# SwiGLU with a 128-byte gap ahead of its tiles, and with one weight split moved between the quarters of the gated parts

## The chip, the cores and the metric

The kernel runs on one core of one Trainium2 chip. The metric is device time in microseconds (us) of one execution of the whole program, the median of several runs. TensorE (PE in the profile) multiplies matrices, and its weight loads have a row of their own (PEld); VectorE is DVE, ScalarE is ACT, GpSimd is POOL, and SP only issues transfers.

## The reference, cut to what matters

The program is a two-layer decoder trunk on 512 tokens of width 1024, all in float32: a recurrent layer with its feed-forward part, then a dilated attention layer with its own feed-forward part. The change touches only the feed-forward part, which is run twice:

```python
def swiglu(h, w_in, w_out):              # h: 512 x 1024, hidden width 2816
    g, u = jnp.split(h @ w_in, 2, axis=-1)
    return (jax.nn.silu(g) * u) @ w_out
```

## The kernel before, in words

**Every product is three matmuls.** A float32 operand is split into a high part (rounded to the fp32r type of TensorE) and a low part (the rest). `mm3` at lines 161 to 165 then issues high times high (L163), high times low (L164, L165), with the first operand held in the array (the stationary one, which the weight load brings in) and the second streamed past it (the moving one). In the profile's names `ps<-gh,wh` the moving operand stands first and the stationary one second. Nearly all matmuls here have a stationary tile of 128x128 and a moving tile of 128x512.

**The stream of weights.** `Stream` (line 74) keeps weight pieces of 128x1024 floats. `_load` brings a piece from HBM into one of two raw buffers `wr`; `_split` makes its high part `wh` with a copy on ScalarE (L117) and its low part `wl` with a subtraction on VectorE (L124). There are three buffers each of `wh` and `wl`. `get(i)` is called just before the matmuls that use piece i, and first splits all pieces up to i + 2 (`asp` is 2 inside the feed-forward part). So the split of piece i + 3 is written into the program only at the `get` of piece i + 1.

**The feed-forward part.** `swiglu` (line 575) computes the first product in five quarters of 512 hidden columns and a plain remainder of 256 columns. A quarter uses a seven-product scheme on 2x2 blocks (`product`, line 739): combinations of the input, split into high and low parts, are the stationary operands, and combinations of the weights are the moving ones. Four of the input combinations (B11, B21, B22, T4) lie in the tiles `xh` and `xl` of the trunk's own pool; three (T1, T2, T3) lie in three tiles of the feed-forward pool, named T in the profile. The gated result of a quarter is transposed by VectorE into `wt`, and sixteen transfers (`land`, line 722) bring it into `gl`. `parts_of` (line 733) then makes its high part `gh` (a copy on ScalarE, L736) and its low part, in `gl` itself (a subtraction on VectorE, L737), in four quarters of 128x512 each. `out_block` (line 770) multiplies them by the second weight matrix: there the weights are stationary, and `gh` and `gl` are the moving operands. For the last quarter no `gh` and `gl` are used: the tiles T1 and T2 take the gated result, so that T is the moving operand in the last eight output blocks (line 814).

**The order.** Within `swiglu` all five engines run in the order in which the code issues (the manual schedule at line 788). The order of a quarter is a string (lines 40 to 42). In the middle ones it is "S1.T1 GA.B11 GB.B21 L S2.T2 O O S3.T3 O S4.B22 O UB.T4", where a name with a dot is a product of 24 matmuls, O is an output block of 24 matmuls, and L is `parts_of` for the quarter before. At an L the pieces for the following product S2 are already split, and the piece of the first O behind it is not: its split is written at the first `get` of S2, behind the four copies and four subtractions of the L. The two engines therefore do, in this order: for GB the additions (L707) and Silu (L708) of `gate`; the four quarters of L736 and L737; then L117 and L124 for the piece of the first O. Four quarters of each feed-forward part begin with such an L, eight in the program. The last quarter has a second L, behind two O, for the gated result that lies in T1 and T2.

**Where tiles lie.** A pool places its tiles in the order in which the code first asks for them, and a tile that is asked for and never used takes its place too. Sizes in bytes of a partition: the trunk's pool (h, xh, xl, constants) and the weights' pool (`wr`, `wh`, `wl`) hold only multiples of 512, so all of these start at the same address modulo 512; call that residue 0. The pool of the second feed-forward part follows directly. That of the first follows the pool "tables", whose tiles, with an unused one of 64 at its start (line 867), come to 64 + 1280 + 3072 + 3x64 + 512 + 1024 = 6144, twelve times 512. So both begin at residue 0. The order inside is: T1, T2, T3 and wt (8192 each), six temporaries e (4096 each), GA, GB, S1 (8192 each), then three small tiles of the norm in two buffers of 64 each (384 together), then S3, UB (8192 each), rb (3072), gh and gl (8192 each). Hence T, wt, e, GA, GB and S1 are at residue 0, and S3, UB, rb, gh and gl at residue 384. All slices that a matmul reads begin at multiples of 512 bytes within their tile.

Of the kernel before, what the change touches and what calls it, by code (L numbers as in the profile page):

```python
# [15 lines left out]
F32 = mybir.dt.float32  # L16
# [22 lines left out]

MIDDLE = "S1.T1 GA.B11 GB.B21 L S2.T2 O O S3.T3 O S4.B22 O UB.T4"  # L40
ORDERS = ["GA.B11 GB.B21 O S1.T1 S2.T2 O S3.T3 S4.B22 UB.T4", MIDDLE, MIDDLE, MIDDLE,
          "S1.T1 GA.B11 GB.B21 L S2.T2 O S3.T3 S4.B22 UB.T4 O O L O"]

C_AN, C_AF, C_KV, C_BN, C_BF, C_CB, C_GA, C_GX, C_LAM, C_CW = [8 * i for i in range(10)]
N_PAR = C_CW + 32
# [28 lines left out]
class Stream:  # L74
# [63 lines left out]
    def load_to(self, i):  # L138
        while self.nl < min(len(self.pieces), i + 1):
            for step in self._load(self.nl):  # L140
                step()
            self.nl += 1

    def prefetch(self, i):
        n = len(self.pieces)
        self.load_to(i + self.al)
        while self.ns < min(n, i + self.asp + 1):
            for step in self._split(self.ns):
                step()
            self.ns += 1  # L150

    def get(self, i):
        self.prefetch(i)
# [3 lines left out]
def trunk(tc, A, out):  # L157
# [11 lines left out]
    def add_pieces(aps, kind="", but=0):  # L169

        start = len(pieces)
        pieces.extend((a, "" if but and i % but == 0 else kind) for i, a in enumerate(aps))
        return start
# [7 lines left out]
    class Ffn:  # L181


        def __init__(self, wi, wo, gain):
            self.gain = gain
            self.wi, self.wo = A[wi], A[wo]
            self.split = None
            self.steps = []
            for j in range(2):
                self.steps += [("plain", j, b, add_pieces([self.wi[b]])) for b in (j, HB + j)]  # L190
            for q, names in enumerate(ORDERS):
                waiting = list(range(0, 8, 2 if q else 4))
                for name in names.split():
                    if name == "O":
                        m = waiting.pop(0)
                        if q:
                            w = self.wo[m:m + 2, :, 512 * q - 256:512 * q + 256]
                        else:
                            w = self.wo[m:m + 4, :, :256]
                        self.steps.append(("out", q, m, add_pieces([w.rearrange("b q c -> q b c")])))  # L200
                    elif name == "L":
                        self.steps.append(("parts",))
                    else:
                        first = len(pieces)
                        for kk in range(2):
                            pieces.append((None, lambda hi, lo, *a: self.split(*a, hi, lo), q, name, kk))
                        self.steps.append(("product", q, name, first))
            self.last = [add_pieces([self.wo[m][:, 128 * (HB - 4):128 * HB]]) for m in range(8)]
# [12 lines left out]
    with tc.tile_pool(name="keep", bufs=1) as kp, tc.tile_pool(name="wts", bufs=3) as wp, \  # L221
            tc.tile_pool(name="ps", bufs=1, space=PSUM) as pp:
        kp, wp = Pool(kp), Pool(wp)
        ws = Stream(tc, nc, wp, pieces, 2, 1)
# [113 lines left out]
        with tc.tile_pool(name="lru", bufs=2) as lp, \  # L338
# [50 lines left out]
            parts = [ws.get(0), ws.get(1)]  # L389
# [158 lines left out]
            for ms in ((0, 1), *((m,) for m in range(2, 8))):  # L548
                parts = [ws.get(p_aout + m) for m in ms]
# [25 lines left out]
        def swiglu(fp, p, after, meanwhile=iter(())):  # L575
            ws.asp, ws.al = 2, 9
            temps = Temps(fp)

            def chunk():
                return [fp.tile([128, 4, T], F32R, name=n, bufs=1) for n in ("gh", "gl")]  # L580
# [149 lines left out]
                        (nc.gpsimd if a == 0 else nc.sync).dma_start(  # L730
                            lo[32 * b:32 * b + 32, :, 128 * a:128 * a + 128].bitcast(F32), src[32 * a:32 * a + 32, :, b])

            def parts_of():
                hi, lo = chunks[max(chunks)]
                for m in range(4):
                    S.copy(hi[:, m], lo[:, m].bitcast(F32))  # L736
                    V.tensor_tensor(lo[:, m], lo[:, m].bitcast(F32), hi[:, m].bitcast(F32), ALU.subtract)  # L737

# [48 lines left out]
            E = mybir.EngineType  # L787
# [19 lines left out]
            with tc.manual_schedule(engines={mybir.EngineType.PE}):  # L807
                for ms in ((0, 1), *((m,) for m in range(2, 8))):
                    parts = [ws.get(p.last[m]) for m in ms]
# [9 lines left out]
        with tc.tile_pool(name="tables", bufs=1) as rp:  # L819
            rp = Pool(rp)  # L820
            with tc.tile_pool(name="ffn1", bufs=2) as fp:
                fp = Pool(fp)
                tables = []

                def make_tables():
                    tables.extend((yield from rotary(nc, A, rp, fp)))

                def after_f1(m, ps):
                    V.tensor_tensor(by_time(h[m]), by_time(h[m]), in_turn(ps), ALU.subtract)
                    split(h[m], gain(C_KV, m), xh[m], xl[m])  # L830
                    squares(m, Temps(fp))

                swiglu(fp, p_f1, after_f1, make_tables())


            with tc.tile_pool(name="att", bufs=2) as ap:
                ap = Pool(ap)
                attention(tc, A, ap, ws, dict(locals()))

        with tc.tile_pool(name="ffn2", bufs=2) as fp:  # L840
            fp = Pool(fp)

            def after_f2(m, ps):

                halves = [(slice(0, 2), nc.scalar), (slice(2, 4), nc.sync)]
                for c, queue in halves if m == 7 else [(slice(0, 4), nc.sync)]:
                    x = by_time(h[m])[:, :, c]
                    V.tensor_tensor(x, x, in_turn(ps)[:, :, c], ALU.subtract)
                    c = slice(128 * c.start, 128 * c.stop)
                    queue.dma_start(out[m][:, c], h[m][:, c])  # L850

            swiglu(fp, p_f2, after_f2)
# [534 lines left out]
```

## Time and profile before

| what | value |
|---|---|
| median of 3 runs (lowest to highest) | 1164.31 us (1163.48 to 1164.59) |
| the profiled execution's own time | 1163.49 us |
| its span, first to last instruction | 1161.4 us |
| PE busy | 1151.7 us, 99% |
| PEld busy | 951.7 us, 82% |
| DVE busy | 851.1 us, 73% |
| ACT busy | 623.2 us, 54% |
| POOL busy | 186.2 us, 16% |
| granted TensorE clock, mean | 0.999 |

The span is cut by the profile into instructions of each engine. A matmul's row gives its modelled duration, about 0.39 us here, and consecutive matmuls overlap: the next one starts about 0.23 us after the one before. So the cost of a matmul to the program is the step from its start to the next start, and a matmul whose modelled duration is 5 ns longer also makes the next one start about 5 ns later. In a row of groups stand line, engine, operation, names, shapes and count, and behind the bar the busy time in us and the mean in ns. In a row of the timeline stand start and duration in us.

### The profile page before, as it was taken

How to read it: one execution, taken by the hardware profiler on the slowest of the kernel's cores; microseconds unless marked ns; L12 is line 12 of the kernel's file. 1: busy time of each engine (PE TensorE's matmuls, PEld its weight loads, DVE VectorE, ACT ScalarE, POOL GpSimd, SP SyncE). 2: the span in 40 equal slices, each digit the busy share in tenths (PEclk: the TensorE clock that was granted, in tenths of full speed). 3: DMA queues.
4: the chain of work that ended last, by engine and by line, in shares of the span. 5: the costliest groups of instructions: out<-in, count | busy, mean ns of one | idle time of the engine just before them, and what ended most of it. 6: DMA issues, size and time to landing. Idle time of an engine off the chain costs nothing.

```text
span 1161.4 us, 15131 instructions
## 1 busy us (share of the span) xinstructions
PE 1151.7 (99%) x5403; PEld 951.7 (82%) x5403; DVE 851.1 (73%) x1525; ACT 623.2 (54%) x901; POOL 186.2 (16%) x221
## 2 busy tenths in 40 slices
PE   9999999999999999999999999999999999999998
PEld 6788888888888888888888888898888888888887
DVE  7988678868777676887565667765888676676764
ACT  6797455553535353665555768665555435353522
POOL 4210010201001000020411234341102011011000
PEclk9999999999999999999999999999999999999999
DMA  7644366966665722333988658535669665657324
GB/s 242 152 113 113 101 227 161 242 190 162 179 174 167 196 73 77 123 104 92 218 191 173 156 104 199 117 74 110 224 162 229 188 163 180 177 164 194 77 65 134
DMA packets 92234, 179.61 MB, mean 155 GB/s; under 512 B 8704, under 2 KB 27008, under 8 KB 92160
## 3 DMA queue, kind: packets, MB, share of 16 engines
q1 hardware_dynamic: 72720, 130.80, 34.9%
q0 software_dynamic: 18864, 47.19, 23.0%
q8 instruction: 43, 0.70, 0.2%
q10 hardware_dynamic: 576, 0.66, 0.2%
q14 instruction: 31, 0.25, 0.1%
HBM read 164.99 MB, written 2.10 MB: 144 GB/s over the span
## 4 chain that ended last, share of the span: by engine, by line
PE 94%; DVE 2%; ACT 1%; DMA 1%; issue 1%; POOL 0%; ACTq 0%; DVEq 0%; SPq 0%
PE ps L165 25%; PE ps L164 25%; PE ps L163 25%; PE ps L1048 6%; PE ps L1049 6%; PE ps L1050 6%; PE ps L1216 1%; PE ps L1134 1%; DVE xc L451 1%; DMA h<-in_x 0%; PE ps L296 0%; DMA wr<-in_w_in 0%; ACT pr L1202 0%; DVE xp L441 0%; PE ps L1102 0%
## 5 line engine op out<-in xcount | busy, mean ns | idle before, releaser
L117 ACT CAST wh<-wr 128x1024 fp32r<-128x1024 f32 (+2 forms) x136 | 131.2, 970 | 135.8 <-PE ps L164 81.0
L164 PE MATMUL ps<-wl,xh 128*128 128x512 f32 x320 | 124.6, 389 | 0.0
L165 PE MATMUL ps<-wh,xl 128*128 128x512 f32 x320 | 124.5, 389 | 0.0
L163 PE MATMUL ps<-wh,xh 128*128 128x512 f32 x320 | 124.5, 389 | 0.0
L165 PE MATMUL ps<-gh,wl 128*128 128x512 f32 x288 | 114.5, 398 | 0.3
L163 PE MATMUL ps<-gh,wh 128*128 128x512 f32 x288 | 113.6, 395 | 0.0
L164 PE MATMUL ps<-gl,wh 128*128 128x512 f32 x288 | 113.6, 394 | 0.0
L124 DVE TENSOR_TENSOR wl<-wr,wh 128x1024 fp32r<-128x1024 f32 (+2 forms) x93 | 100.0, 1084 | 16.8 <-ACT wh L117 16.4
L649 POOL DMA_DIRECT2D S<-in_f_in x40 | 48.2, 1247 | 368.9 <-DMA S<-in_f_in 186.6
L163 PE MATMUL ps<-xh,wh 128*128 128x512 f32 x256 | 101.0, 396 | 0.6 <-ACT xh L274 0.6
L663 ACT CAST wh<-S 128x1024 fp32r<-128x1024 f32 x60 | 63.0, 1050 | 70.4 <-PE ps L165 27.9
L164 PE MATMUL ps<-xl,wh 128*128 128x512 f32 x256 | 100.2, 391 | 0.1
L165 PE MATMUL ps<-xh,wl 128*128 128x512 f32 x256 | 99.8, 390 | 0.0
L664 DVE TENSOR_TENSOR wl<-S,wh 128x1024 fp32r<-128x1024 f32 x60 | 73.2, 1222 | 31.4 <-ACT wh L663 31.4
L163 PE MATMUL ps<-wh,T 128*128 128x512 f32 x240 | 93.5, 390 | 0.0
L165 PE MATMUL ps<-wh,T 128*128 128x512 f32 x240 | 93.5, 390 | 0.0
L164 PE MATMUL ps<-wl,T 128*128 128x512 f32 x240 | 93.4, 389 | 0.0
L1048 PE MATMUL ps<-wh,xh 128*128 128x512 f32 x224 | 91.5, 408 | 0.0
L1050 PE MATMUL ps<-wh,xl 128*128 128x512 f32 x224 | 87.7, 391 | 0.0
L1049 PE MATMUL ps<-wl,xh 128*128 128x512 f32 x224 | 87.3, 390 | 0.0
L781 DVE TENSOR_TENSOR h<-h,ps 128x512 f32<-128x512 f32 x64 | 43.3, 685 | 54.9 <-PE ps L165 54.9
L163 PEld LDWEIGHTS ps<-wh,xh 128*128 128x128 f32 x320 | 60.1, 188 | 12.6
(284 smaller groups left out, 2669.5 us busy)
## 6 DMA issues: line engine op xcount, KB each, us to landing
S<-in_f_in SPq DMA_DIRECT2D x40, 512.0 KB, 6.4
S<-in_f_in POOLq DMA_DIRECT2D x40, 512.0 KB, 9.0
wr<-in_f_out SPq DMA_DIRECT2D x36, 512.0 KB, 5.3
wr<-in_w_q SPq DMA_DIRECT2D x28, 512.0 KB, 6.5
wl<-in_w_q POOLq DMA_DIRECT2D x28, 512.0 KB, 7.7
GA<-in_f_in SPq DMA_DIRECT2D x20, 512.0 KB, 4.9
GB<-in_f_in SPq DMA_DIRECT2D x20, 512.0 KB, 7.0
UB<-in_f_in SPq DMA_DIRECT2D x20, 512.0 KB, 5.3
```

Source lines behind the costliest of these rows:

```text
L117: nc.scalar.copy(hi[:, c], r[:, c])
L124: a = eng.tensor_tensor(lo[:, c], r[:, c], hi[:, c].bitcast(F32), ALU.subtract)
L163: PE.matmul(ps, wh, xh, start=first, stop=False, skip_group_check=on)
L164: PE.matmul(ps, wh, xl, start=False, stop=False, skip_group_check=on)
L165: PE.matmul(ps, wl, xh, start=False, stop=last, skip_group_check=on)
L649: nc.gpsimd.dma_start(c, p.part(1, q, n == "S1", i), accum_op=ALU.add)
L663: S.copy(hi, r)
L664: V.tensor_tensor(lo, r, hi.bitcast(F32), ALU.subtract)
L781: V.tensor_tensor(by_time(x), by_time(x), in_turn(ps), ALU.subtract)
L1048: PE.matmul(ps[t], xh[k][:, r], wh[:, c], start=k == 0, stop=False)
L1049: PE.matmul(ps[t], xh[k][:, r], wl[:, c], start=False, stop=False)
L1050: PE.matmul(ps[t], xl[k][:, r], wh[:, c], start=False, stop=k == 7)
```

## The change

Two edits. The first asks, at the start of `swiglu`, for a tile of 32 floats per partition (128 bytes) that nothing uses. The second adds to `Stream` a method that splits the next piece, and has `parts_of` call it between its second and its third quarter at every L of the order strings. The last quarter's second L becomes an E, which does the quarters as before and splits nothing. No other order and no transfer is written differently.

```diff
-          "S1.T1 GA.B11 GB.B21 L S2.T2 O S3.T3 S4.B22 UB.T4 O O L O"]
+          "S1.T1 GA.B11 GB.B21 L S2.T2 O S3.T3 S4.B22 UB.T4 O O E O"]
...
+    def split_one(self):
+        for step in self._split(self.ns):
+            step()
+        self.ns += 1
+
     def prefetch(self, i):
         n = len(self.pieces)
         self.load_to(i + self.al)
         while self.ns < min(n, i + self.asp + 1):
-            for step in self._split(self.ns):
-                step()
-            self.ns += 1
+            self.split_one()
...
-                    elif name == "L":
-                        self.steps.append(("parts",))
+                    elif name in "LE":
+                        self.steps.append(("parts", name == "L"))
...
         def swiglu(fp, p, after, meanwhile=iter(())):
             ws.asp, ws.al = 2, 9
             temps = Temps(fp)
+            fp.tile([128, 32], F32, name="gap", bufs=1)
...
-            def parts_of():
+            def parts_of(split_next):
                 hi, lo = chunks[max(chunks)]
                 for m in range(4):
+                    if m == 2 and split_next:
+                        ws.split_one()
                     S.copy(hi[:, m], lo[:, m].bitcast(F32))
                     V.tensor_tensor(lo[:, m], lo[:, m].bitcast(F32), hi[:, m].bitcast(F32), ALU.subtract)
```

By the order of requests the gap moves every tile of the two feed-forward pools by 128 bytes: T, wt, e, GA, GB and S1 from residue 0 to 128, and S3, UB, rb, gh and gl from 384 to 512, which is residue 0.

## The prediction

> **What bounds the kernel now.** I read the engines' busy times first, then TensorE's groups by shape, and then one place in the timeline.
>
> ```profile
> PE 1151.7 (99%) x5403; PEld 951.7 (82%) x5403; DVE 851.1 (73%) x1525; ACT 623.2 (54%) x901; POOL 186.2 (16%) x221
> ```
>
> TensorE is busy for all but 10 us of the span. A change can only help by making a matmul's step shorter or by taking away one of the few waits. So the groups of matmuls (busy us, mean ns of one):
>
> ```profile
> core 0 of [0], span 1161.4 us
> line engine op names shapes xcount | busy us, mean ns | idle before us <-releasers
> L164 PE MATMUL ps<-wl,xh 128*128 128x512 f32 x320 | 124.6, 389 | 0.0
> ...
> L165 PE MATMUL ps<-gh,wl 128*128 128x512 f32 x288 | 114.5, 398 | 0.3
> L163 PE MATMUL ps<-gh,wh 128*128 128x512 f32 x288 | 113.6, 395 | 0.0
> L164 PE MATMUL ps<-gl,wh 128*128 128x512 f32 x288 | 113.6, 394 | 0.0
> ...
> L163 PE MATMUL ps<-wh,T 128*128 128x512 f32 x240 | 93.5, 390 | 0.0
> L165 PE MATMUL ps<-wh,T 128*128 128x512 f32 x240 | 93.5, 390 | 0.0
> L164 PE MATMUL ps<-wl,T 128*128 128x512 f32 x240 | 93.4, 389 | 0.0
> ...
> L164 PE MATMUL ps<-T,wh 128*128 128x512 f32 x64 | 24.9, 389 | 0.0
> ```
>
> The same shape costs 389 to 390 ns everywhere, except where the gated product is the moving operand: 394 to 398 ns. That holds whether transfers run beside it or not. Here are two stretches, first by engine (the last two columns are DMA share and GB/s), then one group of matmuls from each:
>
> ```profile
> 185.60:191.10 5.50, 5.50 (x25) 4.42 (x24) 3.72 (x5) 2.28 (x3) 0.00 (x0) 1.00 0.04 7
> 267.50:272.20 4.70, 4.70 (x22) 3.85 (x21) 2.48 (x5) 1.98 (x2) 0.00 (x0) 1.00 1.02 256
> ```
>
> ```profile
> L163 PE MATMUL ps<-gh,wh 128*128 128x512 f32 x8 | 3.2, 395 | 0.0
> ```
>
> ```profile
> L163 PE MATMUL ps<-wh,xh 128*128 128x512 f32 x6 | 2.3, 390 | 0.0
> ```
>
> In the first stretch DMA is at 0.04 and gh matmuls take 395 ns. In the second DMA is at 1.02 and the xh ones take 390 ns, at the same granted clock of 1.00. Nor is it the code of the output block: with T in gh's place the same block takes 389 ns. What is left is where gh and gl lie. They are the only operands of such matmuls whose residue (384) is not that of the operand on the other side (0); T and xh stand at 0 like the weights.
>
> The other thing is a wait at every L. Matmul starts at the first one:
>
> ```profile
> 245.57 0.39 PE L165 MATMUL ps<-wh,T 128*128 128x512 f32 x1
> 245.80 0.39 PE L163 MATMUL ps<-gh,wh 128*128 128x512 f32 x1
> 246.03 0.40 PE L164 MATMUL ps<-gl,wh 128*128 128x512 f32 x1
> 246.47 0.50 PE L165 MATMUL ps<-gh,wl 128*128 128x512 f32 x1
> 246.81 0.39 PE L163 MATMUL ps<-gh,wh 128*128 128x512 f32 x1
> 247.04 0.39 PE L164 MATMUL ps<-gl,wh 128*128 128x512 f32 x1
> ...
> 249.83 0.39 PE L164 MATMUL ps<-gl,wh 128*128 128x512 f32 x1
> ```
>
> The third matmul of the first output block starts 0.44 us after the second, and the fourth 0.34 us after the third, where a step is otherwise 0.23. Among those who waited for the raw weights' split stands, over the whole program:
>
> ```profile
>   PEld ps L165: 3.7, 8
> ```
>
> The weight load of that third matmul waits for `wl`, eight times, once per L. ScalarE and VectorE at the same place:
>
> ```profile
> 242.03 2.17 ACT L736 CAST gh<-gl 128x512 fp32r<-128x512 f32 x4
> 244.11 2.00 ACT L117 CAST wh<-wr 128x1024 fp32r<-128x1024 f32 x2
> ```
>
> ```profile
> 242.67 2.50 DVE L737 TENSOR_TENSOR gl<-gl,gh 128x512 fp32r<-128x512 f32 x4 [1.31 <-ACT gh L736]
> 245.19 2.36 DVE L124 TENSOR_TENSOR wl<-wr,wh 128x1024 fp32r<-128x1024 f32 x2
> 248.03 1.22 DVE L664 TENSOR_TENSOR wl<-S,wh 128x1024 fp32r<-128x1024 f32 x1 [0.49 <-ACT wh L663]
> ```
>
> VectorE begins the first `wl` at 245.19, only when all four quarters of gl are done, and at 2.36 / 2 = 1.18 us each ends it at 246.37. The matmul that needs it would have started at 246.03 + 0.23 = 246.26. The second `wl` is for a later block and not yet needed.
>
> **The change part by part. First, the split between the quarters.** It adds no instruction and no transfer; it moves one L117 and one L124 ahead of the last two quarters. ScalarE's copies step by (244.11 - 242.03) / 4 = 0.52 us, VectorE's subtractions by (245.19 - 242.67) / 4 = 0.63. ScalarE then does two quarters from 242.03, the weights from 243.07 to 244.1, and the other two quarters until 245.2; its second weight copy then ends at 244.11 + 2.00 = 246.11, as before. The copy needs the third `wh` buffer, free since the last matmul of GB; Silu, ahead on the same engine, already waits for GB's results, so no new wait arises. VectorE does two quarters until 243.93, idles until `wh` is there at about 244.15, makes `wl` until 245.35, and the last quarters until 245.98 and 246.61. Who waits for those? The weight load needs `wl` at 246.26: 0.9 us early. The moving gl of k = 2 is needed seven steps after 245.80, at 247.4, and is there at 245.98; that of k = 3 at 248.07, there at 246.61. The second `wl` ends at 246.61 + 1.18 = 247.79, before VectorE's next work at 248.03, which waits for ScalarE anyway. The raw buffer comes free about a microsecond sooner, so SP issues its reload sooner; nothing on that queue is pushed back. So the whole wait goes: 0.44 + 0.34 - 2 x 0.23 = 0.32 us, eight times, **-2.6 us**. Bounds: if only the late start counts, 8 x 0.21 = 1.7; if the part that the weight load waited came back whole, 3.7, of which I keep 3.0, since two starts show less.
>
> **Second, the gap, for gh and gl.** They come to the weights' residue. Their 864 matmuls took 113.6 + 113.6 + 114.5 = 341.7 us, of which 8 x 0.11 = 0.9 is the long third one above; 340.8 / 864 = 394.4 ns against 389.3. By starts, 247.04 to 249.83 is 12 steps of 232.5 ns, and undisturbed steps of products are 227 (the last fence below). The difference is 5.1 to 5.5 ns; I take 5.3: 864 x 5.3 = **-4.6 us**.
>
> **Third, the gap, for T.** It moves T from residue 0 to 128, away from the weights. T is stationary in 720 matmuls (three rows of 240) and moving in 192. The trace shows no matmul of this shape with such a pair, so I bound it. Is the loss a matter of the moving operand's own address, or of the pair? The steps just behind a group of gh matmuls speak for the pair:
>
> ```profile
> 257.26 0.40 PE L163 MATMUL ps<-wh,T 128*128 128x512 f32 x1
> ...
> 259.57 0.39 PE L164 MATMUL ps<-wl,T 128*128 128x512 f32 x1
> 259.80 0.39 PE L165 MATMUL ps<-wh,T 128*128 128x512 f32 x1
> ...
> 262.07 0.39 PE L163 MATMUL ps<-wh,T 128*128 128x512 f32 x1
> ```
>
> Both pairs of rows span ten steps inside one product whose operands are all at residue 0. The first ten take 2.31 us, the second ten 2.27. Whatever gh disturbs outlasts gh by ten matmuls: a phase between the two streams, the moving operand and the weights being loaded, rather than a property of gh's address. Of gh against the weights, the moving operand starts 128 bytes below the stationary one, modulo 512. Of the weights against the moved T, the moving one (0) again starts 128 below the stationary one (128). It is the same pair, shifted. So I price it like gh: 720 x 5.3 = **+3.8 us**; from below, nothing (+0). Where T is moving, it stands 128 above the weights, the other way round, which no row shows: between 0 and 192 x 5.3 = 1.0; I take the middle, **+0.5 us**. The other moved tiles (wt, e, GA, GB, S1, S3, UB, rb) are read and written by VectorE, ScalarE and transfers, which have slack except at an L, where it is about 1 us; I price them at nothing.
>
> **Sum:** -2.6 - 4.6 + 3.8 + 0.5 = -2.9 us. The profiled execution had 1163.49 us, span 1161.4 and about 2 around it, which the change leaves; it would become 1160.6. It lies 0.8 below the median shown, 1164.31, and the same difference there gives **1161.4 us**. With the bounds of the wait (-3.0 to -1.7), of the step (5.1 to 5.5 ns on a net 144 matmuls, 0.7 to 0.8) and of the moving T (0 to 1.0), the likeliest case reaches from 1160.5 to 1163.0.
>
> The Trainium skill says of TensorE, in "TensorE: Matmul & The Clock Gate", section "Step-by-step: what each phase is for", that it has two independent read ports, so that loading the next tile's weights takes no read bandwidth from the running matmul. By that rule no residue could matter between the two streams, and only the wait would go. The rows of gh (394 to 398 ns against 389) don't fit it unless something else slows gh.
>
> **The rivals.**
>
> *A stationary operand may lie anywhere.* If only the moving operand's address counts, T costs nothing in the 720. Then -2.6 - 4.6 + 0.5 = -6.7 us: 1157.6 (1157.1 to 1158.1 with the two ends for the moving T). For it: every slow row has gh or gl as the moving operand. Against it: the ten slow steps behind gh.
>
> *The residue is not the cause, or the gap takes no place.* Then the change does half of what it says, and gh stays at 394 ns for a reason not seen here. Only the wait goes: 1164.31 - 2.6 = 1161.7. Against it: T in the same code at 389 ns, and quiet and busy transfers alike. That an unused tile takes its place shows in the first feed-forward part, where T comes right only with the 64 unused bytes of "tables".
>
> *Slower: T pays more than gh did.* Weights stream against T in 720 matmuls, with the weight load turning between T's two halves of a product. The change wins 2.6 + 4.6 = 7.2 us elsewhere; spread over 720 + 192 matmuls of T that is 7.9 ns each, and from there it decides. The longest gh matmul was 404 ns:
>
> ```profile
> L163 PE MATMUL ps<-gh,wh x288: 390/393/404, 185.6 to 1135.1; 128*128 128x512 f32 x144
> ```
>
> That is 15 ns above 389; if all of T's ran so, 912 x 15 = 13.7, and the time is 1170.8; at 10 ns it is 1166.2. Against it: none of the three gh groups has a mean above 398 ns, 9 over the rest, and T's pair is gh's own.
>
> **How the numbers follow.** The likeliest case (T pays like gh) has 52%, the free stationary operand 22%, no effect of the residue 13%, slower T 9%; 4% are left for gains and losses that cancel (1164.3). A measurement of this kernel can tell about 0.2%, 2.3 us, from no change, so faster begins below 1162.0 and slower above 1166.6. Of the likeliest case two thirds lie below 1162.0 (35 of 52), of the second all but one (21), of the third 8: 64% faster. Slower is 7 from T and 1 for what I don't see: 8%. The rest, 28%, is no change. The range goes from the second rival's lower end, 1157.0, to 1164.4, past the likeliest case's upper end and the cancelling case; outside are most of the slower rival and a part of the ends.
>
> **What would show it.** The gh and gl rows at 389 to 390 ns; the rows `wh,T` and `wl,T` at about 395 (at 389 the first rival is right, above 398 the last); `T,wh` between 389 and 395; no PEld waiting eight times for `wl`, and steps of 0.23 us at the first O behind each L. If gh stays at 394, the residue is wrong. If the gaps at the L remain, look whether ScalarE's copy of the weights started late. The prediction is wrong most easily at the price of T's new residue, which stands on one pair seen the other way round.

## The result, and the profile after

The changed kernel takes 1160.79 us (1160.62 to 1162.09), beside 1163.48 us (1162.55 to 1165.77) for the kernel before on the same chip: a ratio of 0.9978, 95% interval 0.9969 to 0.9987, or 2.7 us less. The forecast was 2.9 us less: 1161.4 us, from a median of 1164.31.

The page of the changed kernel, its first line:

```profile
span 1158.7 us, 15131 instructions
```

The span is 2.7 us shorter with the same number of instructions. The groups of TensorE by shape (the lines of `mm3` are three higher than before):

```profile
L168 PE MATMUL ps<-gh,wl 128*128 128x512 f32 x288 | 112.2, 389 | 0.0
L167 PE MATMUL ps<-gl,wh 128*128 128x512 f32 x288 | 112.1, 389 | 0.0
L166 PE MATMUL ps<-gh,wh 128*128 128x512 f32 x288 | 112.0, 389 | 0.0
...
L166 PE MATMUL ps<-wh,T 128*128 128x512 f32 x240 | 94.9, 396 | 0.0
L168 PE MATMUL ps<-wh,T 128*128 128x512 f32 x240 | 94.8, 395 | 0.0
L167 PE MATMUL ps<-wl,T 128*128 128x512 f32 x240 | 94.7, 395 | 0.0
...
L168 PE MATMUL ps<-T,wl 128*128 128x512 f32 x64 | 25.3, 395 | 0.0
L166 PE MATMUL ps<-T,wh 128*128 128x512 f32 x64 | 25.3, 395 | 0.0
L167 PE MATMUL ps<-T,wh 128*128 128x512 f32 x64 | 25.3, 395 | 0.0
```

The rows of gh and gl, which stood between 394 and 398 ns, are down at 389. Those of T went from 389 or 390 up to 395 or 396, as the stationary and as the moving operand alike. The slowness has changed its place. Now the first output block behind the first L, as the starts of its matmuls:

```profile
245.62 0.39 PE L166 MATMUL ps<-gh,wh 128*128 128x512 f32 x1
245.85 0.40 PE L167 MATMUL ps<-gl,wh 128*128 128x512 f32 x1
246.08 0.39 PE L168 MATMUL ps<-gh,wl 128*128 128x512 f32 x1
246.31 0.39 PE L166 MATMUL ps<-gh,wh 128*128 128x512 f32 x1
...
248.35 0.39 PE L166 MATMUL ps<-gh,wh 128*128 128x512 f32 x1
```

The steps of 0.44 and 0.34 us are gone; all are 0.23. From 246.31 to 248.35 are nine steps of 227 ns, where the kernel before had 232.5. VectorE at the same place:

```profile
242.33 1.29 DVE L743 TENSOR_TENSOR gl<-gl,gh 128x512 fp32r<-128x512 f32 x2 [1.32 <-ACT gh L742]
243.80 1.23 DVE L124 TENSOR_TENSOR wl<-wr,wh 128x1024 fp32r<-128x1024 f32 x1 [0.18 <-ACT wh L117]
244.95 1.29 DVE L743 TENSOR_TENSOR gl<-gl,gh 128x512 fp32r<-128x512 f32 x2
```

The first `wl` is done at 245.03, 1.05 us before the matmul that needs it; the last quarters of gl end at 246.24. Over the whole program, those who waited for the split of the raw weights are now these, and no PEld is among them:

```profile
  POOL wl L121: 127.0, 32
  ACT wh L117: 27.0, 11
  DVE wl L124: 18.1, 40
```

A useful clock for all that follows is the length of a middle quarter, from the first gh matmul behind one L to the first behind the next. It holds seven products and four output blocks, 11 x 24 = 264 matmuls, of which 72 have T stationary and 96 have gh or gl moving. The next such start, before and after:

```profile
306.60 0.39 PE L163 MATMUL ps<-gh,wh 128*128 128x512 f32 x1
```

```profile
305.96 0.39 PE L166 MATMUL ps<-gh,wh 128*128 128x512 f32 x1
```

Before it is 306.60 - 245.80 = 60.80 us, after it is 305.96 - 245.62 = 60.34.

### The profile page after: what moved, and what is told of

It is laid out like the page before. It is cut to its first block, busy times and chain, and to the rows that moved or that the text cites. A ratio compares the mean times of both kernels' runs of the same rounds, so it can differ in the third digit from the quotient of the medians.

```text
span 1158.7 us, 15131 instructions
## 1 busy us (share of the span) xinstructions
PE 1150.0 (99%) x5403; PEld 953.4 (82%) x5403; DVE 851.0 (73%) x1525; ACT 622.9 (54%) x901; POOL 187.7 (16%) x221
## 4 chain that ended last, share of the span: by engine, by line
PE 94%; DVE 2%; ACT 1%; issue 1%; POOL 0%; DMA 0%; SPq 0%; DVEq 0%; ACTq 0%
PE ps L168 25%; PE ps L167 25%; PE ps L166 25%; PE ps L1054 6%; PE ps L1055 6%; PE ps L1056 6%; PE ps L1222 1%; PE ps L1140 1%; DVE xc L454 1%; PE ps L299 0%; DMA wr<-in_w_in 0%; ACT pr L1208 0%; PE ps L1108 0%; ACT wh L117 0%; DVE wl L124 0%
## 5 line engine op out<-in xcount | busy, mean ns | idle before, releaser
L168 PE MATMUL ps<-gh,wl 128*128 128x512 f32 x288 | 112.2, 389 | 0.0
L167 PE MATMUL ps<-gl,wh 128*128 128x512 f32 x288 | 112.1, 389 | 0.0
L166 PE MATMUL ps<-gh,wh 128*128 128x512 f32 x288 | 112.0, 389 | 0.0
L166 PE MATMUL ps<-wh,T 128*128 128x512 f32 x240 | 94.9, 396 | 0.0
L168 PE MATMUL ps<-wh,T 128*128 128x512 f32 x240 | 94.8, 395 | 0.0
L167 PE MATMUL ps<-wl,T 128*128 128x512 f32 x240 | 94.7, 395 | 0.0
L787 DVE TENSOR_TENSOR h<-h,ps 128x512 f32<-128x512 f32 x64 | 43.3, 685 | 49.6 <-PE ps L168 49.1
```

Of the source, the lines that this page charges most:

```text
L166: PE.matmul(ps, wh, xh, start=first, stop=False, skip_group_check=on)
L167: PE.matmul(ps, wh, xl, start=False, stop=False, skip_group_check=on)
L168: PE.matmul(ps, wl, xh, start=False, stop=last, skip_group_check=on)
L787: V.tensor_tensor(by_time(x), by_time(x), in_turn(ps), ALU.subtract)
```

## The experiments

### The two edits apart

The split alone leaves out this line of the change:

```diff
-            fp.tile([128, 32], F32, name="gap", bufs=1)
```

> The split between the quarters alone, without the gap. Theory (the prediction's sum): the eight waits go and nothing else, 8 x 0.32 = 2.6 us less than the kernel before; gh and gl rows stay at 394 ns, T rows at 389 to 390. Rival (the split's place gains little, and nearly all of the change's 2.7 us came from the gap): less than 0.7 us less, and steps at the first output block behind an L that are still 0.44 and 0.34 us.

Measured: 1160.92 us against 1163.8 for the kernel before, ratio 0.9974 (0.9964 to 0.9985), 2.9 us less. One row of its groups and two starts:

```profile
L166 PE MATMUL ps<-gh,wh 128*128 128x512 f32 x288 | 113.7, 395 | 0.0
```

```profile
245.73 0.40 PE L166 MATMUL ps<-gh,wh 128*128 128x512 f32 x1
...
306.23 0.40 PE L166 MATMUL ps<-gh,wh 128*128 128x512 f32 x1
```

gh stays at 395 ns, and the quarter is 60.50 us: 0.30 less than before, where 0.32 was priced. So the split alone is as fast as the whole change.

The gap alone adds only that line to the kernel before.

> The gap alone, without the split. Theory (gh and T pay alike, by the pair): 864 x 5.3 = 4.6 us won at gh, (720 + 192) x 5.3 = 4.8 us lost at T, so within 0.5 us of the kernel before; the eight waits stay. Rival (the gap is what made the change faster): about 2.7 us less than before.

Measured: 1163.16 us, ratio 0.9994 (0.9985 to 1.0003): no difference that can be told, 0.6 us by the medians. The wait is still there, but shorter:

```profile
245.55 0.39 PE L163 MATMUL ps<-gh,wh 128*128 128x512 f32 x1
245.78 0.40 PE L164 MATMUL ps<-gl,wh 128*128 128x512 f32 x1
246.06 0.50 PE L165 MATMUL ps<-gh,wl 128*128 128x512 f32 x1
246.40 0.40 PE L163 MATMUL ps<-gh,wh 128*128 128x512 f32 x1
```

```profile
306.07 0.39 PE L163 MATMUL ps<-gh,wh 128*128 128x512 f32 x1
```

The two steps are 0.28 and 0.34, so the wait costs 0.28 + 0.34 - 2 x 0.23 = 0.16 us instead of 0.32. The product S2.T2, which runs while the weights are split, has T stationary. Its 24 matmuls are now 6 ns slower each, 0.14 us in all, and `wl` is that much less late: VectorE ends it at 245.96, 0.41 us after the first of these starts, where it was 246.37 - 245.80 = 0.57 us in the kernel before. The quarter is 306.07 - 245.55 = 60.52. So in the changed kernel, with its quarter of 60.34, the split is worth 0.18 us per quarter and not 0.32.

### Both operands in place

The gap is asked for behind T, just ahead of rb; the split stays:

```diff
             temps = Temps(fp)
-            fp.tile([128, 32], F32, name="gap", bufs=1)
...
                 elif b == HB:
+                    fp.tile([128, 32], F32, name="gap", bufs=1)
                     rows[:] = [spread(*rows, fp.tile([128, 768], F32, name="rb", bufs=1)[:, :T], S.copy)]
```

> Split and gap, but the gap is asked for just before rb, behind T, wt, e, GA, GB, S1, S3 and UB: T stays at residue 0 and gh and gl come to residue 0 as well. Theory (every pair at one residue is fast): gh, gl and T rows all at 389 to 390 ns, 2.6 + 4.6 = 7.2 us less than before, 4.5 less than the changed kernel. Rival (gh became fast for another reason than its own residue, such as the moved raw weights GA and S1 or the temporaries): gh stays at 394 ns and only the 2.6 us of the waits are won.

Measured: 1155.37 us, ratio 0.9926 (0.9913 to 0.9938), 8.4 us less than before. This version beats both kernels.

```profile
L166 PE MATMUL ps<-gh,wh 128*128 128x512 f32 x288 | 112.0, 389 | 0.0
...
L166 PE MATMUL ps<-wh,T 128*128 128x512 f32 x240 | 93.4, 389 | 0.0
```

```profile
246.63 0.39 PE L166 MATMUL ps<-gh,wh 128*128 128x512 f32 x1
...
306.47 0.39 PE L166 MATMUL ps<-gh,wh 128*128 128x512 f32 x1
```

All rows of gh, gl and T are at 389 ns, and the quarter is 59.84 us, 264 steps of 226.7 ns with nothing between them. It won 1.2 us more than the 7.2 expected. Against the split alone the quarter lost 60.50 - 59.84 = 0.66 us; over the 96 matmuls of gh and gl that is 6.9 ns each, where 5.3 was priced. Over all 864 matmuls of the two traces the mean step of gh and gl went from 233.1 to 226.7 ns, so 6.4 of it is their own, more than the twelve steps and the rows of the kernel before told. The rest is the disturbance that outlasts gh in the products behind it.

### Is it the pair or the address?

The same kernel with every tile 128 bytes higher:

```diff
+        kp.tile([128, 32], F32, name="shift")
         h = [kp.tile([128, T], F32, name=f"h{k}") for k in range(KB)]
```

> The kernel with the gap behind T, and 128 unused bytes at the start of the trunk's own pool, so that every tile of the program lies 128 bytes higher, all operands of the matmuls at one common residue that differs from before. Theory (only the difference between the moving and the stationary operand's residue counts): all rows as with the gap behind T, 389 to 390 ns, time within 0.5 us of it. Rival (the absolute residue of an operand counts): all the matmuls of 512 columns, some 4600, pay 5 ns, and the time is 23 us longer than with the gap behind T.

Measured: 1154.79 us, ratio 0.9924 (0.9912 to 0.9937).

```profile
245.01 0.39 PE L166 MATMUL ps<-gh,wh 128*128 128x512 f32 x1
...
304.85 0.39 PE L166 MATMUL ps<-gh,wh 128*128 128x512 f32 x1
```

The rows of gh, gl and T are at 389 ns and the quarter is 59.84 us again. Moving all operands together by 128 bytes changes nothing, while moving T or gh alone by 128 does; so it is the operands' difference that counts.

### How the price goes with the distance

In both kernels here gh and gl stay at residue 0, and an unused tile ahead of T sets T's residue, another one in each feed-forward part. For the first of the two:

```diff
             temps = Temps(fp)
+            shift = 64 if p is p_f1 else 256
+            fp.pool.tile([128, shift // 4], F32, name="gap_t", bufs=1)
...
+                    fp.pool.tile([128, (640 - shift) // 4 % 128 or 128], F32, name="gap", bufs=1)
```

> The kernel with the gap behind T (gh and gl at residue 0), and T moved: to residue 64 in the first feed-forward part, to 256 in the second. How does the price go with the distance? Theory (any unequal residue costs the same): T rows at about 395 ns in both parts, so 912 x 6 ns = 5.5 us longer than with the gap behind T alone. Rival (only a distance of 128 to either side collides, four places of 128 bytes modulo 512): T rows at 389 ns at 256, and nearly so at 64; the time within 1.5 us of the gap behind T.

Measured: 1158.33 us, ratio 0.9953 (0.9930 to 0.9975). T's groups in the first part (T at 64), then in the second (T at 256):

```profile
L166 PE MATMUL ps<-wh,T 128*128 128x512 f32 x120 | 47.5, 396 | 0.0
...
L167 PE MATMUL ps<-T,wh 128*128 128x512 f32 x32 | 12.6, 394 | 0.0
```

```profile
L166 PE MATMUL ps<-wh,T 128*128 128x512 f32 x120 | 46.7, 389 | 0.0
...
L167 PE MATMUL ps<-T,wh 128*128 128x512 f32 x32 | 12.5, 389 | 0.0
```

Both theories fall. With T stationary a distance of 64 costs as much as 128, and a distance of 256 costs nothing in either role. So the residue that counts is modulo 256, not 512. With T moving, 64 costs less: the row of T with wl was at 389 ns and the other two at 393 and 394. Why is open.

The second kernel has 32 and 384 in place of 64 and 256.

> As the run before, with T at residue 32 in the first feed-forward part and at 384 in the second. With T at 384 the stationary T stands 128 below the moving weights, the other sign than in the changed kernel. Theory (any unequal residue costs the same): T rows at about 395 ns in both. Rival (the price grows with the distance or depends on the sign): T rows nearer to 389 ns at 32, and at 384 other values for the stationary and the moving T than the 395 of the changed kernel.

Measured: 1161.7 us, ratio 0.9983 (0.9972 to 0.9994). T at 32, then T at 384:

```profile
L167 PE MATMUL ps<-wl,T 128*128 128x512 f32 x120 | 47.4, 395 | 0.0
...
L166 PE MATMUL ps<-T,wh 128*128 128x512 f32 x32 | 12.7, 395 | 0.0
```

```profile
L167 PE MATMUL ps<-wl,T 128*128 128x512 f32 x120 | 47.4, 395 | 0.0
...
L166 PE MATMUL ps<-T,wh 128*128 128x512 f32 x32 | 12.6, 395 | 0.0
```

32 costs the full price in both roles, and so does 384. For 384 that is what modulo 256 says, since it is then 128. The times agree with the rows: 8.4 us less than before with both parts of T in place, 5.8 with one (the kernel with 64 and 256), 2.4 with none.

### Own weights or the next ones?

With the gap behind T, 128 unused bytes stand between the buffers of `wh` and of `wl`:

```diff
         hi = self.pool.tile([128, 1024], F32R, name=f"wh{i}", tag="wh")
+        if i == 0:
+            self.pool.tile([128, 32], F32, name="apart", bufs=1)
         lo = self.pool.tile([128, 1024], F32R, name=f"wl{i}", tag="wl")
```

> Which of a matmul's neighbours makes the pair: the weights already in the array, or the ones loaded while it runs? The kernel with the gap behind T, and 128 unused bytes between the buffers of wh and those of wl. Now xh, xl and wh are at residue 0, and wl, T, gh, gl and all that lies behind are at 128. In the first layer's first product xh and xl move and the weights are stationary, in turn xh with wh, xl with wh, xh with wl. Theory one (the load of the next weights collides with the stream): xl with wh is slow, since wl is loaded while it runs, at about 395 ns, and xh with wl is fast. Theory two (the own weights count): xh with wl is slow and xl with wh is fast. In the output blocks gh and gl move at 128: by theory one gh with wh and gh with wl are slow and gl with wh fast; by theory two gh with wh and gl with wh are slow and gh with wl fast. If the disturbance lasts several matmuls whatever began it, all three rows lie between. Longer in all than with the gap behind T: a third to two thirds of the first layer's 768 and of the 864 matmuls, the 720 with T stationary and the weights' high part moving, and the 320 with xh stationary and wl moving pay about 6 ns, some 8 to 12 us.

Measured: 1176.19 us, ratio 1.0103 (1.0074 to 1.0132), 20.8 us longer than with the gap behind T in the other comparison, about twice what was expected.

```profile
L168 PE MATMUL ps<-wh,xh 128*128 128x512 f32 x320 | 126.9, 397 | 0.0
L169 PE MATMUL ps<-wl,xh 128*128 128x512 f32 x320 | 126.4, 395 | 0.0
L170 PE MATMUL ps<-wh,xl 128*128 128x512 f32 x320 | 125.5, 392 | 0.0
L170 PE MATMUL ps<-gh,wl 128*128 128x512 f32 x288 | 114.1, 396 | 0.0
L169 PE MATMUL ps<-gl,wh 128*128 128x512 f32 x288 | 113.7, 395 | 0.0
L168 PE MATMUL ps<-gh,wh 128*128 128x512 f32 x288 | 113.4, 394 | 0.0
```

Neither theory has its fast row here: all three rows of gh pay 5 to 7 ns. The rows in which `xh` and `xl` move, for which the two theories were set apart, are these; they hold the first layer's product and the other products of that form:

```profile
L170 PE MATMUL ps<-xh,wl 128*128 128x512 f32 x256 | 102.2, 399 | 0.0
L169 PE MATMUL ps<-xl,wh 128*128 128x512 f32 x256 | 102.1, 399 | 0.1
L168 PE MATMUL ps<-xh,wh 128*128 128x512 f32 x256 | 102.0, 400 | 0.8 <-ACT xh L279 0.8
```

In the kernel moved as a whole they were at 390, 391 and 396. So `xh,wl`, whose own weights lie apart, and `xl,wh`, during which such weights are loaded, are both slow; their median step is 234 and 232 ns. That of `xh,wh`, whose mean holds a few long matmuls in both kernels, stays at 227, and its row pays least. Here either of the two seems to be enough. But the row `wh,xh` above has its own operands at residue 0, and the weights loaded beside it too, and is the slowest of its three at 397. And where T is stationary the other way round happens:

```profile
L168 PE MATMUL ps<-wh,T 128*128 128x512 f32 x240 | 94.2, 393 | 0.0
L170 PE MATMUL ps<-wh,T 128*128 128x512 f32 x240 | 93.8, 391 | 0.0
L169 PE MATMUL ps<-wl,T 128*128 128x512 f32 x240 | 93.2, 389 | 0.0
```

`wl,T`, both at 128, pays nothing between two rows of unequal residues, and these pay 4 and 2 ns, not 6. A matmul can thus pay for residues that belong to its neighbours, and need not; no rule tried here covers all of these rows, and whether the own weights or the next ones begin the loss stays open.

## Why the prediction was right, and where its sizes were off

**The forecast held:** 2.9 us less was said, 2.7 was measured, and the likeliest case was the one that happened.

**The split.** Priced at 2.6 us for eight waits; alone it measured 2.9 us and 0.30 us per quarter. The reordered work ran as worked out: `wl` 1.05 us early (0.9 was said). What the sum missed is that the edits share this term. With the gap, the product ahead of the wait is slower and the wait is only 0.16 us, so the split adds 0.18 us per quarter there, eight quarters with an L making about 1.4 us, not 2.6; the other 1.3 is won by the gap itself.

**gh and gl.** Priced at 4.6 us. The three groups went from 341.7 to 112.2 + 112.1 + 112.0 = 336.3 us, that is 5.4, of which 0.9 was the long third matmul of the wait: 4.5. By starts it is more: over both whole traces the 864 steps took 201.4 us with the split alone and 196.1 with the gap added, 5.3 us or 6.1 ns each. The modelled durations understate the step here, so this term was priced too small.

**T stationary.** Priced at 3.8 us on the ground that it is gh's pair shifted by 128. The groups went from 280.4 to 94.9 + 94.8 + 94.7 = 284.4: 4.0. The kernel moved as a whole shows that this ground was sound: the difference counts. That it is a matter of the moving operand and of the weights being loaded beside it, as the prediction says, is not shown; the run with `wl` apart leaves that open.

**T moving.** Priced at 0.5, between 0 and 1.0. It measured 3 x (25.3 - 24.9) = 1.2 us, outside the bound. The step that failed is the middle between two ends: the other sign is no other case, since 128 above and 128 below are the same modulo 256.

**How the terms add up.** Added from start to next start over both traces, the matmuls of gh and gl, which hold the waits too, took 203.6 us before and 196.1 after: 7.5 less, where 2.6 + 4.6 = 7.2 was priced. T stationary took 163.6 and 167.6, T moving 43.3 and 44.6: 5.3 more, where 4.3 was priced. That leaves 2.2 us. The other 0.5 lies in matmuls which the change does not touch, and these scatter: the matmuls with `xh` and `xl` moving in `mm3` alone took between 178.5 and 180.0 us in the kernels before, changed, and of the first four experiments. So the terms were off by 0.3 us one way and 1.0 the other, and the untouched matmuls made up for most of it. The terms were the right ones, with the right signs; that the forecast came within 0.2 us is luck.

**One reading was too wide.** The prediction says that this shape costs 389 to 390 ns everywhere but at gh and gl. In the kernel before, the rows `xh,wh` (396), `wh,xh` of line 1048 (408) and `wh,xp` (404) have the same shape and are longer still. Their medians are 389, so a few long matmuls of up to 499 ns make these means, while all of `gh,wh` lie at 390 or above with a median of 393. The three rows stay where they are after the change (398, 408, 404), so they took nothing from the sum.

**The rivals.** A stationary operand that may lie anywhere is refuted by T at 395 ns. That the residue is not the cause is refuted by the gap behind T: 5.5 us less than the split alone, by nothing but the addresses of the tiles behind the gap. T paying more than gh did not come: 395 or 396 ns against gh's 394 to 398. The rule of the Trainium skill ("TensorE: Matmul & The Clock Gate", section "Step-by-step: what each phase is for"), that loading the next weights takes no read bandwidth from the running matmul, would, as the prediction applied it, give the gap behind T the time of the split alone. The trace does not show that: 389 ns against 395 for the same matmuls. Whether it is read bandwidth that the slow ones lose, no run here shows.

## What to carry to other kernels

When TensorE runs without gaps and one group of matmuls is a few ns slower than others of its shape, compare where its operands begin: here the moving and the stationary ones had to be equal modulo 256 bytes. Look at the median too, since a few long matmuls raise a mean as well. An unused tile that repairs one operand moves everything behind it, so list all operands of matmuls before choosing its place. Price two edits together where one slows the work that hides the other's wait.

## What the runs showed of the hardware that was not expected

In the feed-forward parts a matmul of 128x512 in fp32r took 389 ns in its row and stepped at 226.7 ns when all operands were equal modulo 256. A difference of 32, 64, 128 or 384 bytes cost about 6 ns, hardly depending on its size, but for a moving T at 64, which cost 0 to 5; 256 cost nothing, nor did moving all tiles by 128. Weights with two residues in turn (`wh` and `wl` 128 apart) cost 20.8 us over the program; some matmuls with both operands at one residue paid 8 ns there, and others nothing.
